# Small experts: gate and up split over TensorE's column quarters by output column, with a buffer and PSUM banks of their own

## The chip, the core and the metric

One core of a Trainium2 chip runs the program. The metric is the device time of one execution in microseconds; the kernel before was timed in three runs. One further execution was profiled, and every row below is from it.

## What is computed

Two decoder layers on 256 tokens of width 1024, all in float32. The part that the change touches is the channel sub-layer of the second layer, a top-2-of-8 mixture of SwiGLU experts with D_FF = 2816:

```
logits = h @ router;  top_val, top_idx = top_k(logits, 2);  gate = softmax(top_val) scattered over 8 experts
out = sum over e of  gate[:, e] * ((silu(h @ w_gate[e]) * (h @ w_up[e])) @ w_down[e])
x   = layer_norm(alpha * x + (1 + g2) * out)
```

## The kernel before

The experts' weights lie in HBM as `moe_units`: 33 units of 1 MB for each expert, that is, for each of the 11 blocks `b` of 256 hidden columns two units of gate and up (one per half of the 1024 rows, laid out as row tile, gate or up, column) and one of down. All 264 units are streamed once, through a ring of 7 buffers of 1 MB that SyncE (SP) fills in order (`moe_raw`, L1404; its DMAs are issued at L1411 and L1416). SP waits at each issue until the buffer's last reader is done.

The router sorts the experts by tokens and picks one of six written-out programs (`PLANS`). The rows below are from the first: three large experts (place 7 with room for 128 tokens, places 0 and 1 with 192) and five small ones (places 6 to 2, 32 tokens each, in the code `WHOLE`). A plan's last tuple says how many slots of small experts are woven into each large expert: 12, 72 and 72 of the 165; what is left runs behind the last large expert. A slot is half a unit of a large expert or a whole unit of a small one.

`experts` (L1776) writes the instructions out in that order under `manual_schedule`. It walks through the slots; ahead of each it calls `tick`, which lets every open generator write one more step. The generators in `procs` (one `glu` per block) all advance; those in `back` only the first (`back_whole`, `scatter_whole`, `scatter` wait in line there), and one `gather` beside them. A generator that finds no scratch bank (`banks`, class Banks) or no room (`t2`, `backs`, `yys`) writes nothing in that tick. Where a slot cannot go on, `until` calls `tick` over and over, and all that the generators then write stands on the engines ahead of the slot.

Large experts: ScalarE copies each half unit to rounded float32 (L1930), VectorE subtracts to get the rest (L1933), and TensorE makes two or three products of 512 columns per token tile (`products`, L1612: L1615, L1616, L1618). Sums lie in banks B and C. `empty` copies a finished expert's four down sums to four buffers `yy` (L1688, then GpSimd at L1690) and `scatter` adds them to the tokens' rows (L1705 to L1722). The next large expert's first product waits until `empty` is written (`full`).

Small experts, in plain float32, which TensorE runs as two passes for each matmul:

- `work_whole` (L1959), gate and up: four matmuls for a unit, one per row tile `a`, each with 32 stationary columns (the tokens) and 512 moving ones, on the four column quarters of the array (L1969). Each quarter so holds a part of the sum over rows for all 512 columns; the four parts must still be added.
- `glu_whole` (L1537): ScalarE copies the 128x512 bank (L1543), four matmuls with `ident4` add the four quarters and turn them (L1549), ScalarE takes silu (L1553), VectorE multiplies by up (L1555).
- down (L1978): four matmuls of 512 columns on the four quarters, into a bank of tag A. The two A banks take turns.
- `empty_whole` (L2038) multiplies the sum by the gain into one of the four `yy` (L2042), `back_whole` (L1566) builds the rows that carry the tokens back (VectorE L1575 and L1579, four transposes L1588, ScalarE L1593) and needs a `yy` too while it does, and `scatter_whole` (L1597) makes four matmuls of 128x512 (L1605), each followed by VectorE's add (L1608).

The four `yy` are thus shared between `empty` (all four at once for 192 tokens), `empty_whole` and `back_whole`. Scratch banks are D and, when no small gate/up sum needs it soon, one B.

`end` (L1725) adds the last small expert (L1736, L1740), normalises and writes out. `rest` (L2226) scales and shifts the residual on GpSimd (L2231, eight instructions of 128x512).

Of the kernel before, what the change touches and what calls it, by code (L numbers as in the profile page):

```python
# [18 lines left out]
D = 1024  # L19
KT = 8  # L20
# [83 lines left out]
class Trunk:  # L104
    def __init__(self, tc, ctx, io):
# [6 lines left out]
        self.aside = 0  # L112

    def bank(self, tag="B"):
        return self.ps.tile([128, 512], F32, tag=tag, name="bank" + tag, bufs={"A": 2, "B": 3, "C": 2, "D": 1}[tag])
# [1133 lines left out]
    def open_moe(self, mo):  # L1249
        self.mx = mo  # L1250
        self.nt2 = 3
# [10 lines left out]
        self.chunks = [c[:, i] for i in range(4)] + [mo.tile([128, KT, 128], F32R, name="xg2")]  # L1262

# [5 lines left out]
    def moe_consts(self):  # L1269
# [12 lines left out]
        nc.vector.tensor_reduce(self.ident4, self.ident.rearrange("p (g n) -> p n g", n=WHOLE), axis=AX.X, op=OP.add)  # L1282
        self.rw = cp.tile([128, KT, 8], F32, name="rw")
# [144 lines left out]
    def gather(self, wanted, xH, xL, out, pos=None, banks=None, t2=None, backs=None):  # L1428
# [58 lines left out]
        for s, w, ch in tiles:  # L1487
# [10 lines left out]
            t = mx.tile([128, SEQ], F32R, tag="selT", name="selT", bufs=8)  # L1498
# [67 lines left out]
    def back_whole(self, place, out, banks, backs, yys):  # L1566
# [5 lines left out]
        while not yys.take():  # L1572
            yield
        sel = self.sums().rearrange("p (t n) -> p t n", t=NT)
        nc.vector.memset(sel, 0.0)  # L1575
        for tt in range(NT):
            for hf in range(2):
                s = sel[:, tt, 128 * hf:128 * hf + 128].rearrange("p (i h n) -> p i h n", h=2, n=WHOLE)[:, :, hf, :]
                nc.vector.tensor_scalar(s, self.iota[:, 0:WHOLE].unsqueeze(1).to_broadcast([128, 2, WHOLE]),  # L1579
# [773 lines left out]
```

## Time and profile before

| | |
|---|---|
| timed runs | 1449.87, 1452.04, 1452.89 us; median 1452.04 |
| profiled execution | 1455.61 us, its span 1453.8 us |
| busy in the span: TensorE, VectorE, ScalarE, GpSimd | 91%, 58%, 43%, 16% |
| granted TensorE clock, mean | 0.956 of full speed |
| moved by DMA | 398.31 MB, 274 GB/s over the span |
| experts, first product to the end | 688.7 to 1453.8 us |

How to read it: the expert part is half the span, and it has stages with different limits, so shares of the whole span say little. The windows below cut it where the large experts begin and end. A row of the view of windows gives, for each stretch, its length, the busy time and instruction count of each engine, the granted clock, the mean busy share of the 16 DMA engines and GB/s. In the timeline, a matmul's time is its latency; how fast matmuls follow each other is read from their starts. A float32 matmul counts as two (a transpose as one).

### The profile page before, as it was taken

The page shows a single profiled execution, that of the slowest core. Times are in us where ns is not written, and L with a number is a line of the kernel's source. Part 1 is how long each engine was busy: PE and PEld are TensorE (multiplying, and loading weights), DVE is VectorE, ACT ScalarE, POOL GpSimd, SP SyncE. Part 2 cuts the span into 40 slices and gives each one's busy share as a digit, 9 for nine tenths or more (in the row PEclk, how much of TensorE's full clock was granted, in tenths as well). Part 3 has the DMA queues.
Part 4 walks back from the last instruction along what each step waited for, and adds up shares of the span by engine and source line. Part 5 has one row for each costly group of instructions (what it writes and reads, how often), then busy time and mean ns, then how long its engine had stood idle before and what let it go on. Part 6 is the DMA issues. An engine that isn't in the chain of part 4 may idle for free.

```text
span 1453.8 us, 21710 instructions
## 1 busy us (share of the span) xinstructions
PE 1329.3 (91%) x8070; PEld 929.4 (64%) x8070; DVE 844.9 (58%) x1691; ACT 621.6 (43%) x1179; POOL 232.5 (16%) x284
## 2 busy tenths in 40 slices
PE   5599998799999789997899999999998999999974
PEld 1457746789998567556677666666655666665622
DVE  7956568987776575656867644444434444444224
ACT  2342544455554314633676534344334344443311
POOL 5562015234000331012300100000002000000012
PEclk9799999899999899998999999999999999999977
DMA  9465743356666648533699999999994999999930
GB/s 328 126 180 161 263 112 119 117 189 219 230 232 203 189 144 277 202 95 138 219 354 375 420 418 417 414 404 410 421 421 174 382 411 412 393 422 398 415 124 31
DMA packets 123969, 398.31 MB, mean 274 GB/s; under 512 B 21256, under 2 KB 74848, under 8 KB 84944
## 3 DMA queue, kind: packets, MB, share of 16 engines
q1 hardware_dynamic: 123248, 396.21, 72.7%
q8 instruction: 65, 1.06, 0.3%
q0 software_dynamic: 608, 0.64, 0.2%
q14 instruction: 48, 0.39, 0.1%
HBM read 395.77 MB, written 1.05 MB: 273 GB/s over the span
## 4 chain that ended last, share of the span: by engine, by line
PE 39%; issue 10%; DVE 2%; POOL 1%; ACT 1%; ACTq 0%; POOLq 0%; DVEq 0%
PE bankB L1615 5%; PE bankB L1616 5%; PE bankC L1615 4%; PE bankC L1969 4%; PE bankC L1616 4%; PE bankB L1618 4%; PE bankA L1978 3%; PE bankB L1969 2%; PE bankC L1618 1%; PE bankD L1549 1%; PE bankB L1549 1%; PE bankB L1526 0%; PE bankD L1716 0%; PE bankD L1643 0%; DVE sel L1513 0%
## 5 line engine op out<-in xcount | busy, mean ns | idle before, releaser
L147 DVE TENSOR_TENSOR L<-raw,H 128x512 fp32r<-128x512 f32 (+1 forms) x241 | 167.3, 706 | 68.2 <-ACT H L143 66.2
L143 ACT ACTIVATE H<-raw 128x512 fp32r<-128x512 f32 (+1 forms) x244 | 144.4, 602 | 134.7 <-PE bankB L153 84.4
L1933 DVE TENSOR_TENSOR early<-raw,early 128x1024 fp32r<-128x1024 f32 x120 | 146.4, 1234 | 89.1 <-ACT early L1930 86.4
L153 PE MATMUL bankB<-hHL,H 128*128 128x256 f32 (+1 forms) x560 | 162.2, 290 | 11.7 <-DVE hHL L395 11.7
L152 PE MATMUL bankB<-hHL,H 128*128 128x256 f32 (+1 forms) x560 | 161.8, 290 | 9.5 <-ACT hHL L394 9.5
L154 PE MATMUL bankB<-hHL,L 128*128 128x256 f32 (+1 forms) x560 | 162.7, 291 | 4.3 <-DVE L L147 4.2
L1930 ACT ACTIVATE early<-raw 128x1024 fp32r<-128x1024 f32 x120 | 123.8, 1050 | 13.1 <-DMA raw<-in_moe_units_dram 9.1
L153 PEld LDWEIGHTS bankB<-hHL,H 128*128 128x128 f32 (+1 forms) x560 | 107.0, 191 | 16.9 <-DVE hHL L395 13.6
L152 PEld LDWEIGHTS bankB<-hHL,H 128*128 128x128 f32 (+1 forms) x560 | 106.6, 191 | 15.2 <-ACT hHL L394 9.8
L1615 PE MATMUL bankB<-early,xg 128*128 128x512 f32 x264 | 113.6, 430 | 1.7 <-ACT xg L1481 1.7
L154 PEld LDWEIGHTS bankB<-hHL,L 128*128 128x128 f32 (+1 forms) x560 | 107.0, 191 | 8.9 <-DVE L L147 5.5
L1616 PE MATMUL bankB<-early,xg 128*128 128x512 f32 x264 | 105.2, 399 | 1.0 <-DVE early L1933 1.0
L1618 PE MATMUL bankB<-early,xg 128*128 128x512 f32 x264 | 105.0, 398 | 0.0
L1615 PEld LDWEIGHTS bankB<-early,xg 128*128 128x128 f32 x264 | 50.1, 190 | 59.1 <-issue 29.5
L1690 POOL TENSOR_TENSOR yy<-yy,grow 128x512 f32<-128x512 f32 x10 | 12.6, 1280 | 388.9 <-ACT yy L1688 388.9
L1615 PE MATMUL bankC<-early,xg 128*128 128x512 f32 x176 | 69.5, 395 | 0.0
L1616 PE MATMUL bankC<-early,xg 128*128 128x512 f32 x176 | 69.5, 395 | 0.0
L1933 DVE TENSOR_TENSOR early<-early,early 128x1024 fp32r<-128x1024 f32 x42 | 52.3, 1262 | 25.3 <-ACT early L1930 23.7
L284 PE MATMUL bankD<-raw,cpad 128*32 128x512 f32 x320 | 54.8, 657 | 6.2 <-DMA raw<-in_ada_w_dram 5.8
L1618 PEld LDWEIGHTS bankB<-early,xg 128*128 128x128 f32 x264 | 50.0, 189 | 11.9
L1933 DVE TENSOR_TENSOR early<-ring,early 128x1024 fp32r<-128x1024 f32 x32 | 40.8, 1285 | 28.2 <-ACT early L1930 27.2
L1615 PE MATMUL bankC<-early,eHL 128*128 128x512 f32 x132 | 56.9, 431 | 0.1
(602 smaller groups left out, 2825.3 us busy)
## 6 DMA issues: line engine op xcount, KB each, us to landing
raw<-in_moe_units_dram SPq DMA_DIRECT2D x151, 1024.0 KB, 8.5
early<-in_moe_units_dram SPq DMA_DIRECT2D x76, 1024.0 KB, 8.6
raw<-in_ada_w_dram SPq DMA_DIRECT2D x48, 1024.0 KB, 5.9
ring<-in_moe_units_dram SPq DMA_DIRECT2D x37, 1024.0 KB, 9.0
raw<-in_ffn_w_gate_dram SPq DMA_DIRECT2D x11, 1024.0 KB, 5.3
raw<-in_ffn_w_up_dram SPq DMA_DIRECT2D x11, 1024.0 KB, 5.1
raw<-in_ffn_w_down_dram SPq DMA_DIRECT2D x11, 1024.0 KB, 6.4
raw<-in_w_in_dram SPq DMA_DIRECT2D x16, 512.0 KB, 5.5
```

The source lines that it names most:

```text
L143: i = nc.scalar.activation(Hv, src, AF.Copy)
L147: self.parts = i, (engine or nc.vector).tensor_sub(Lv, src, Hv.bitcast(F32))
L152: mm(out, lh, rh, start=start, stop=False)
L153: mm(out, lh, rl, start=False, stop=False)
L154: self.last = mm(out, ll, rh, start=False, stop=stop)
L284: nc.tensor.matmul(pt[32 * q:32 * q + 32, :], self.cpad[:, k, :], t[:, 512 * q:512 * q + 512], start=(k == 0), stop=(k == KT - 1))
L1615: mm(o, xs[0], wH, start=first, stop=False)
L1616: mm(o, xs[0], wL, start=False, stop=last and w == 64)
L1618: mm(o, xs[1], wH, start=False, stop=last)
L1930: nc.scalar.activation(zv, src, AF.Copy)
L1933: (nc.gpsimd if not whole and n >= len(slots) - 54 and n % 3 == 2 else v).tensor_sub(zv, src, hl[n][1].bitcast(F32))
L1969: nc.tensor.matmul(o.gu[WHOLE * a:WHOLE * a + WHOLE].rearrange("p (g n) -> p g n", g=2), xs[:, 4 * u + a, c:c + WHOLE], t[:, :, a, :], sta ...
```

## The change

Gate and up of a small expert: each quarter now takes 64 of the 256 output columns of both gate and up, for all eight row tiles, so that a unit is 16 matmuls of 128 columns instead of four of 512, and no sum over quarters is left. Gate and up lie side by side on the same partitions. `glu_whole` takes silu out of the bank, multiplies by up, and only then turns the 128x64 product with two matmuls and one copy. The sums of the small experts' down products get a fixed bank V, the second A bank becomes a scratch bank W, and the scaled sum gets a buffer `yw` of its own. `back_whole` builds its rows without a `yy`, from a diagonal matrix, a matmul with ones and a comparison. The shares are 12, 68 and 68. GpSimd's first instruction of `rest` is a copy of one column of `abuf[4]`, which the first large expert's fifth block writes.

```diff
-    ([(7, 128), (0, 192), (1, 192)], [(6, 32), (5, 32), (4, 32), (3, 32), (2, 32)], (12, 72, 72)),
+    ([(7, 128), (0, 192), (1, 192)], [(6, 32), (5, 32), (4, 32), (3, 32), (2, 32)], (12, 68, 68)),
...
-        self.nt2 = 3
+        self.nt2 = 2
...
+        self.late = mo.tile([128, 1], F32, name="late")
...
+        self.slot = cp.tile([128, 2], F32, name="slot")
...
-            t = mx.tile([128, SEQ], F32R, tag="selT", name="selT", bufs=8)
+            t = mx.tile([128, SEQ], F32R, tag="selT", name="selT", bufs=7)
...
-    def glu_whole(self, g, o, banks, t2):
+    def glu_whole(self, g, o, banks):
...
-        while not t2.take():
-            yield
-        z = self.t2([128, 512])
-        nc.scalar.activation(z, g, AF.Copy)
+        z = self.mx.tile([128, 64], F32, tag="zw", name="zw", bufs=2)
+        nc.scalar.activation(z, g[:, 0:64], AF.Silu)
+        yield
+        nc.vector.tensor_mul(z, z, g[:, 64:128])
         yield "read"
...
-        pt = self.bank(bn)[:, 0:4 * WHOLE]
-        for i in range(4):
-            nc.tensor.matmul(pt[:, WHOLE * i:WHOLE * i + WHOLE], z[:, 128 * i:128 * i + 128], self.ident4,
+        pt = self.bank(bn)[:, 0:2 * WHOLE]
+        id4 = self.ident.rearrange("p (i r n) -> p r i n", i=2, r=2)
+        for r in range(2):
+            nc.tensor.matmul(pt[64 * r:64 * r + 64].rearrange("p (i n) -> p i n", i=2), z, id4[:, r],
                              start=True, stop=True)
-        t2.free()
         yield
-        nc.scalar.activation(o, pt[:, 0:2 * WHOLE], AF.Silu)
-        yield
-        nc.vector.tensor_mul(o, o, pt[:, 2 * WHOLE:4 * WHOLE])
+        nc.scalar.activation(o, pt, AF.Copy)
...
-    def back_whole(self, place, out, banks, backs, yys):
+    def back_whole(self, place, out, banks, backs):
...
-        while not yys.take():
-            yield
-        sel = self.sums().rearrange("p (t n) -> p t n", t=NT)
-        nc.vector.memset(sel, 0.0)
+        dg = [self.act.tile([128, 128], F32, tag="dg", name="dg", bufs=2) for _ in range(NT)]
         for tt in range(NT):
...
+            nc.vector.tensor_scalar(dg[tt], self.ident, self.pos[:, tt, place:place + 1], None, op0=OP.mult)
...
+        for tt in range(NT):
+            nc.tensor.matmul(pt[:, 128 * tt:128 * tt + 128], self.ones, dg[tt], start=True, stop=True)
         yield
         for hf in range(2):
-            t = mx.tile([128, SEQ], F32, tag="selT", name="selW", bufs=8)
-            nc.scalar.activation(t, pt[:, 256 * hf:256 * hf + 256], AF.Copy)
+            t = mx.tile([128, SEQ], F32, tag="selT", name="selW", bufs=7)
+            nc.vector.tensor_scalar(t, pt, self.slot[:, hf:hf + 1], None, op0=OP.is_equal)
...
-        banks = Banks("DB", lambda: state["now"], REST)
+
+        self.fixed = {n: self.bank("A") for n in "VW"} if whole else {}
+        step_banks = "DW" if whole else "D"
+        banks = Banks(step_banks + "B", lambda: state["now"], REST)
...
-                for a in range(4):
-                    nc.tensor.matmul(o.gu[WHOLE * a:WHOLE * a + WHOLE].rearrange("p (g n) -> p g n", g=2),
-                                     xs[:, 4 * u + a, c:c + WHOLE], t[:, :, a, :], start=(u == 0), stop=(u == 1))
+                for k in range(4 * u, 4 * u + 4):
+                    for i in range(4):
+                        nc.tensor.matmul(o.gu[WHOLE * i:WHOLE * i + WHOLE, 0:128].rearrange("p (g n) -> p g n", g=2),
+                                         xs[:, k, c:c + WHOLE], t[:, :, k % 4, 64 * i:64 * i + 64],
+                                         start=(k == 0), stop=(k == KT - 1))
             else:
                 if o.b == 0:
-                    Y[o.q] = self.bank("A")
+                    Y[o.q] = self.bank("V")
...
         def empty_whole(q):
-            while not yys.take(1):
+            while not yw.take():
                 yield
-            y = self.sums()
+            y = self.mx.tile([128, 512], F32, tag="yw", name="yw", bufs=1)
             v.tensor_mul(y, Y[q], gain[0])
...
-            banks.names = "D" if any(o.spare and u == 0 for o, u in soon) else "DB"
+            banks.names = step_banks + ("" if any(o.spare and u == 0 for o, u in soon) else "B")
...
         def rest(banks):
 
+            p.tensor_copy(self.late, self.abuf[4][:, 0:1])
             for tt in range(NT):
```

The change moves instructions. Two places matter.

The first is ScalarE where large expert 0 ends and large expert 1 begins. L1472 and L1481 make the tokens of expert 1 ready (`gather`), L1930 rounds a half unit of weights, L1688 empties expert 0's sums. In the kernel before, from the last silu of the small experts on, no half unit is rounded between these steps:

```order
L1553 ACTIVATE sab<-bankB 128x64
L1472 ACTIVATE t_9847<-bankB,colB,colA 128x192 x2
L1481 ACTIVATE xg<-t_9847 128x256
L1481 ACTIVATE xg<-t_9847 128x2x64
L1472 ACTIVATE t_9866<-bankB,colB,colA 128x192 x2
L1481 ACTIVATE xg<-t_9866 128x256
L1481 ACTIVATE xg<-t_9866 128x2x64
L1593 ACTIVATE selW<-bankD 128x256 x2
```

In the changed kernel the same steps (L1484, L1493) stand well ahead of that place, during expert 0's down products, with the rounding (here L1937) and the small experts' silu (L1554) and copy (L1566) between them:

```order
L1484 ACTIVATE t_9753<-bankA,colB,colA 128x192 x2
L1554 ACTIVATE zw<-bankB 128x64
L1493 ACTIVATE xg<-t_9753 128x256
L1493 ACTIVATE xg<-t_9753 128x2x64
L1937 ACTIVATE early_6727<-ring 128x1024 x2
L1681 ACTIVATE eHL<-ab_6741 128x2x128
L1566 ACTIVATE sab<-bankD 128x64
L1681 ACTIVATE eHL<-ab_6741 128x2x64
L1937 ACTIVATE early_6727<-early_6729 128x1024
L1554 ACTIVATE zw<-bankB 128x64
```

The gather of expert 1 moved from one lump at the handover into the stage of expert 0.

The second is TensorE behind the last product of the last large expert. Before, it carries back two small experts (L1588, L1605) ahead of the next units of weights (L1969 gate and up, L1978 down):

```order
L1978 MATMUL bankA<-raw,sab 32x512 x4
L1549 MATMUL bankD<-ident_2373,t_11796 128x32 x4
L1588 MATMUL bankD<-ident,yy_6727 128x128 x4
L1605 MATMUL bankD<-yy_6726,selW 128x512 x4
L1588 MATMUL bankD<-ident,yy_6725 128x128 x4
L1605 MATMUL bankD<-yy_6724,selW 128x512 x4
L1969 MATMUL bankB<-raw,xg_7065 32x512 x8
L1716 MATMUL bankD<-yHL,selT 128x256 x4
L1978 MATMUL bankA<-ring,sab 32x512 x4
L1716 MATMUL bankD<-yHL,selT 128x256 x4
```

Changed, units of weights (L1977, L1987) come at once, and the large expert's scatter (L1719) stands between them:

```order
L1563 MATMUL bankD<-ident,zw 64x64 x2
L1977 MATMUL bankB<-early_6729,xg_7075 32x128 x16
L1977 MATMUL bankB<-raw,xg_7075 32x128 x16
L1719 MATMUL bankD<-yHL,selT 128x256 x4
L1987 MATMUL bankA<-raw,sab 32x512 x4
L1563 MATMUL bankA<-ident,zw 64x64 x2
L1719 MATMUL bankD<-yHL,selT 128x256 x4
L1977 MATMUL bankB<-raw,xg_7075 32x128 x16
L1977 MATMUL bankB<-ring,xg_7075 32x128 x16
L1719 MATMUL bankD<-yHL,selT 128x256 x4
```

The carrying back of the small experts (L1608 in the changed kernel) moved forward, four instructions for each expert spread between products of the large ones, and 17 units instead of 9 are left for this last stretch.

## Rows read from the trace of the kernel before

**Rows 1.** The page: the span, busy time of the engines, and GB/s in 40 equal slices of the span.

```profile
span 1453.8 us, 21710 instructions
...
PE 1329.3 (91%) x8070; PEld 929.4 (64%) x8070; DVE 844.9 (58%) x1691; ACT 621.6 (43%) x1179; POOL 232.5 (16%) x284
...
GB/s 328 126 180 161 263 112 119 117 189 219 230 232 203 189 144 277 202 95 138 219 354 375 420 418 417 414 404 410 421 421 174 382 411 412 393 422 398 415 124 31
```

**Rows 2.** The view of windows: the expert part cut into expert 7 (two rows), expert 0, the handover, expert 1, the stop behind it, the last units, and `end`.

```profile
688.70:704.00 15.30, 9.37 (x37) 6.72 (x38) 11.10 (x13) 8.61 (x9) 13.20 (x8) 0.92 0.23 72
704.00:823.40 119.40, 119.40 (x626) 87.36 (x625) 86.61 (x118) 82.33 (x131) 5.13 (x6) 0.98 0.94 363
823.40:1086.60 263.20, 261.86 (x1504) 167.06 (x1500) 114.35 (x175) 106.43 (x184) 4.86 (x5) 1.00 1.01 415
1086.60:1113.20 26.60, 19.91 (x106) 12.95 (x102) 13.32 (x38) 12.59 (x33) 3.53 (x3) 0.94 0.36 151
1113.20:1382.00 268.80, 266.19 (x1525) 170.66 (x1521) 108.47 (x167) 105.47 (x186) 8.85 (x10) 0.99 0.98 399
1382.00:1411.30 29.30, 19.45 (x56) 6.14 (x55) 7.46 (x14) 4.51 (x11) 5.67 (x5) 0.71 0.23 86
1411.30:1434.90 23.60, 17.13 (x98) 8.94 (x97) 5.77 (x16) 4.42 (x12) 5.08 (x7) 0.80 0.17 71
1434.90:1453.80 18.90, 5.70 (x8) 2.19 (x8) 11.00 (x18) 1.01 (x2) 5.71 (x6) 0.68 0.16 59
```

**Rows 3.** The timeline of TensorE in the stage of expert 0, where a product, a down unit, a `glu_whole`, a gate/up unit and the next product follow each other (start, length, line, shapes, count).

```profile
967.26 1.06 PE L1978 MATMUL bankA<-raw,sab 128*32 128x512 f32 x8
...
968.26 1.08 PE L1549 MATMUL bankD<-ident,t 128*128 128x32 f32 x8
...
969.27 1.06 PE L1969 MATMUL bankC<-ring,xg 128*32 128x512 f32 x8
...
970.26 0.50 PE L1615 MATMUL bankB<-early,xg 128*128 128x512 f32 x1
```

**Rows 4.** The view of windows, stage of expert 0, for the matmuls of line 1549 alone and then of line 1978 alone (eight records per block, and per unit).

```profile
823.40:1086.60 263.20, 22.96 (x184) 23.08 (x184) 1.00 1.01 415
...
823.40:1086.60 263.20, 25.39 (x192) 4.19 (x192) 1.00 1.01 415
```

**Rows 5.** The timeline of ScalarE and VectorE around the same place: silu, multiplication and the copy of a bank in `glu_whole`.

```profile
961.52 0.22 ACT L1553 ACTIVATE sab<-bankB 128x64 f32<-128x64 f32 x1 [0.43 <-PE bankB L1549]
961.77 0.22 DVE L1555 TENSOR_TENSOR sab<-sab,bankB 128x64 f32<-128x64 f32 x1 [1.45 <-ACT sab L1553]
...
962.62 0.60 ACT L1543 ACTIVATE t<-bankC 128x512 f32<-128x512 f32 x1 [0.88 <-PE bankC L1969]
```

**Rows 6.** The timeline of TensorE, three runs of short float32 passes elsewhere in the program: 128 columns in one quarter, 64 columns in two halves, 128 columns in two halves.

```profile
73.34 1.72 PE L684 MATMUL bankC<-early,X 128*32 128x128 f32 x14
...
244.79 1.15 PE L617 MATMUL bankD<-ident,sl 128*64 128x64 f32 x32
...
1102.80 0.66 PE L1495 MATMUL bankB<-ident,sel 128*64 128x128 f32 x8
```

**Rows 7.** The view of windows, the handover from expert 0 to 1, for lines 1458 (`gather`), 1526 (`gather_whole`) and 1605 (`scatter_whole`, two records each) alone.

```profile
1086.60:1113.20 26.60, 4.83 (x32) 3.96 (x32) 0.94 0.36 151
...
1086.60:1113.20 26.60, 4.59 (x24) 4.42 (x24) 0.94 0.36 151
...
1086.60:1113.20 26.60, 7.86 (x14) 2.09 (x14) 0.94 0.36 151
```

**Rows 8.** The timeline at the start of expert 7: GpSimd's `rest`, one of TensorE's waits, and VectorE's subtraction (L1933) and comparison (L1513, four at a time) first beside `rest` and then without it.

```profile
688.74 13.20 POOL L2231 TENSOR_TENSOR x<-x,yy 128x512 f32<-128x512 f32 x8 [15.88 <-ACT xg L1481]
...
695.20 0.50 PE L1616 MATMUL bankB<-early,xg 128*128 128x512 f32 x1 [0.42 <-DVE early L1933]
...
697.30 2.31 DVE L1933 TENSOR_TENSOR early<-raw,early 128x1024 fp32r<-128x1024 f32 x1
699.53 2.75 DVE L1513 TENSOR_SCALAR sel<-iota,posS 128x32 fp32r<-128x32 f32 x4
702.19 1.22 DVE L1933 TENSOR_TENSOR early<-raw,early 128x1024 fp32r<-128x1024 f32 x1
...
703.66 0.67 DVE L1513 TENSOR_SCALAR sel<-iota,posS 128x32 fp32r<-128x32 f32 x4
```

**Rows 9.** The view of waits of SP's DMA queue over the expert part: who was waited for, microseconds in total, times, longest; and the timeline of SP at the handover.

```profile
SPq L1411 <- PE bankC L1969: 49.8, 10, 26.0
...
SPq L1416 <- PE bankB L1969: 44.9, 10, 26.2
...
1086.13 27.63 SPq L1411 DMA_DIRECT2D raw<-in_moe_units_dram  x3
```

**Rows 10.** The timeline behind the last product of the last large expert, and from the view of DMA issues the median from issue to landing of a unit.

```profile
1381.88 27.12 SPq L1416 DMA_DIRECT2D raw<-in_moe_units_dram  x2
...
1384.78 1.12 PE L1605 MATMUL bankD<-yy,selW 128*128 128x512 f32 x2 [0.75 <-ACT selW L1593]
...
1406.71 2.67 PE L1969 MATMUL bankB<-raw,xg 128*32 128x512 f32 x16
...
1427.18 0.58 PE L1716 MATMUL bankD<-yHL,selT 128*128 128x256 f32 x1 [0.57 <-ACT yHL L1705]
...
1429.57 0.58 PE L1716 MATMUL bankD<-yHL,selT 128*128 128x256 f32 x1 [0.57 <-ACT yHL L1705]
...
1434.88 3.78 PE L1740 MATMUL bankB<-yy,selW 128*128 128x512 f32 x4 [0.47 <-ACT selW L1593]
...
raw<-in_moe_units_dram SPq DMA_DIRECT2D x130, 1024.0 KB, 8.8
```

More of the change, by code (lines that the diff above doesn't have):

```diff
@@ L112, in __init__ @@
         self.aside = 0
+        self.fixed = {}
     def bank(self, tag="B"):
+        if tag in self.fixed:
+            return self.fixed[tag]
         return self.ps.tile([128, 512], F32, tag=tag, name="bank" + tag, bufs={"A": 2, "B": 3, "C": 2, "D": 1}[tag])
@@ L1282, in moe_consts @@
         nc.vector.tensor_reduce(self.ident4, self.ident.rearrange("p (g n) -> p n g", n=WHOLE), axis=AX.X, op=OP.add)
+        self.slot = cp.tile([128, 2], F32, name="slot")
+        t = self.mx.tile([128, 512], F32, tag="asb", name="asb", bufs=1)[:, 0:WHOLE]
+        nc.vector.tensor_mul(t, self.ident4, self.iota[:, 0:WHOLE])
+        for hf in range(2):
+            nc.vector.tensor_reduce(self.slot[:, hf:hf + 1], t, axis=AX.X, op=OP.add)
+        for i in range(128 // WHOLE):
+            nc.vector.memset(self.slot[WHOLE * i:WHOLE * i + WHOLE, 1 - i % 2:2 - i % 2], -2.0)
         self.rw = cp.tile([128, KT, 8], F32, name="rw")
@@ L1571, in back_whole @@
             yield
-        while not yys.take():
-            yield
-        sel = self.sums().rearrange("p (t n) -> p t n", t=NT)
-        nc.vector.memset(sel, 0.0)
+        dg = [self.act.tile([128, 128], F32, tag="dg", name="dg", bufs=2) for _ in range(NT)]
         for tt in range(NT):
-            for hf in range(2):
-                s = sel[:, tt, 128 * hf:128 * hf + 128].rearrange("p (i h n) -> p i h n", h=2, n=WHOLE)[:, :, hf, :]
-                nc.vector.tensor_scalar(s, self.iota[:, 0:WHOLE].unsqueeze(1).to_broadcast([128, 2, WHOLE]),
-                                        self.pos[:, tt, place:place + 1], None, op0=OP.is_equal)
+            nc.vector.tensor_scalar(dg[tt], self.ident, self.pos[:, tt, place:place + 1], None, op0=OP.mult)
         yield
@@ L1583, in back_whole @@
             yield
-        pt = self.bank(bn)
-        for hf in range(2):
-            for tt in range(NT):
-                c = 256 * hf + 128 * tt
-                nc.tensor.transpose(pt[:, c:c + 128], sel[:, tt, 128 * hf:128 * hf + 128], self.ident)
-        yys.free()
+        pt = self.bank(bn)[:, 0:SEQ]
+        for tt in range(NT):
+            nc.tensor.matmul(pt[:, 128 * tt:128 * tt + 128], self.ones, dg[tt], start=True, stop=True)
         yield
         for hf in range(2):
-            t = mx.tile([128, SEQ], F32, tag="selT", name="selW", bufs=8)
-            nc.scalar.activation(t, pt[:, 256 * hf:256 * hf + 256], AF.Copy)
+            t = mx.tile([128, SEQ], F32, tag="selT", name="selW", bufs=7)
+            nc.vector.tensor_scalar(t, pt, self.slot[:, hf:hf + 1], None, op0=OP.is_equal)
             out.append(t)
@@ L1853, in experts @@
                 continue
-            kinds = {z.kind for z, _ in slots[max(o.first - NEAR, 0):o.last + NEAR] if z.q in large}
+            kinds = {z.kind for z, _ in slots[max(o.first - NEAR - (AHEAD if whole else 0), 0):o.last + NEAR]
+                     if z.q in large}
             o.spare = kinds != {"u"}
@@ L1895, in experts @@
         place = {n: i for i, n in enumerate([n for n, (o, _) in enumerate(slots) if o.q not in whole])}
-        selW, gain = {}, []
+        selW, gain, yw = {}, [], Room(1)
         procs = []
@@ L1994, in glu @@
             if o.q in whole:
-                work = self.glu_whole(o.gu, parts(o.q, o.b), banks, t2)
+                work = self.glu_whole(o.gu, parts(o.q, o.b), banks)
             else:
@@ L2048, in scatter_whole @@
             yield from self.scatter_whole(q, selW[q], ys[q], acc, banks)
-            yys.free(1)
+            yw.free()
             backs.free(2)
@@ L2115, in after @@
                     if o.b == NB - LATE:
-                        back.append(self.back_whole(o.q, selW.setdefault(o.q, []), banks, backs, yys))
+                        back.append(self.back_whole(o.q, selW.setdefault(o.q, []), banks, backs))
                 elif o.b == NB - 1:
```

2 lines of the change are left out of this document (1 added, 1 removed).

## Prediction

> **What bounds the kernel now.** I read the page first and then the expert part in windows. TensorE is busy for 91% of the span, but the GB/s line says more: from the 23rd slice on it stands near 415, with one hole in the 31st and an end that moves little [rows 1]. So two engines are near full at once. The windows show it stage by stage [rows 2]. In the stage of expert 0 (263.2 us) TensorE is busy for 261.9 us and the DMA engines for the whole of it at 415 GB/s; in that of expert 1 (268.8 us) it is 266.2 us and 399 GB/s. Between and behind them lie two holes: 26.6 us at 151 GB/s at the handover, 29.3 us at 86 GB/s behind the last large product. There the stream of weights stands: SP's two longest waits, 26.0 and 26.2 us, are for gate/up matmuls of small experts [rows 9], which hold the ring's oldest buffers and stand on TensorE behind work that has nothing to do with weights [rows 10]. Then 23.6 us of last units and 18.9 us of `end`.
>
> What sets the pace inside a stage? The reader should compare starts: down unit 967.26, `glu_whole` 968.26, gate/up unit 969.27, product 970.26 [rows 3]. They follow each other without a gap, 1.0 us each. TensorE is thus the one that others wait for, with the DMA right behind: a stage of 72 slots and 33 large units takes in 105 units of 1.049 MB, which at 415 GB/s need 265 us.
>
> All sums below are against the profiled execution; its 1455.61 us are 3.6 us above the median of the timed runs, 1452.04, to which I apply the difference.
>
> **The change part by part.**
>
> *Gate and up, 110 units.* One unit was 4 matmuls of 512 columns on four quarters: 8 passes, 0.99 us from start to next start [rows 3]. Now it is 16 matmuls of 128 columns, 32 passes; each quarter streams 4 x 128 columns as it streamed 512. If the quarters still run at once, the streaming is the same, and only more weight loads and issues could show. No row has 128 columns on four quarters. Near it: 32 passes with their 32 loads took 1.15 us where each was 64 columns on halves [rows 6], so the engine can issue that many in about a microsecond; that is the upper near bound, +0.16 us. The lower bound is a few hundredths below nothing, since the drain at either end is shared. Far bounds: one at a time, 1.72 us for 14 passes, 0.12 a pass and 3.9 us a unit; two at a time half of that, 2.0 us (8 passes on halves took 0.66 us with their latency, 0.08 a pass) [rows 6]. I take +0.05 us, nearest to the four-quarter row, whose geometry it keeps.
>
> *`glu_whole`, 55 blocks.* Eight passes with loads of 128 columns took 1.0 us [rows 3], 22.96 us of busy time for 23 blocks in one stage [rows 4]; where a product follows, about 0.9. Now 4 passes of 64 columns on halves: at the 0.036 us a pass of line 617 [rows 6] 0.14 us, and a change of array shape on both sides for which I add 0.2. I take 0.35, bounds 0.15 and 0.9. ScalarE gives up a 0.60 us copy and gains a 0.22 us one [rows 5]; VectorE's product stays. Both are busy for about 40% of these stages [rows 2], so neither costs anything; if they were full, it would be the 0.2 us of the added copy a block.
>
> *Start of expert 7, 15.3 us.* GpSimd's eight instructions run at 688.74 for 13.2 us, and beside them VectorE's subtraction takes 2.31 instead of 1.22 us and four comparisons 2.75 instead of 0.67; TensorE waits for the subtraction [rows 8] and is busy for 9.4 of 15.3 us [rows 2]. The copy of one column holds GpSimd back until the fifth block is through, some 30 us later, when VectorE has run ahead. I take -5 us here. The rest of expert 7's stage: 5 `glu_whole` save 2.8, ten gate/up units cost 0.5, the moved GpSimd work 1: **-1.3** (bounds -3 and +4, if all of the slowness moves along).
>
> *Stage of expert 0, 263.2 us.* Less: four slots of about 0.95 us, 3.8; 23 `glu_whole` of 0.91 become 22.7 of 0.35, 13.0. More: 45 gate/up units, 2.3. And the work of the handover now lies in here: the gather of expert 1, 4.8 us, that of the last small expert, 4.6, seven products of `scatter_whole` in 14 records, 7.9 [rows 7], less some 0.6 since the clock was 0.94 there and will be 1.00; the selection matrices 1.3 and `back_whole` 0.5. Sum **+3.2**. Its DMA floor is 101 units, 255 us; TensorE still sets the pace with 266.
>
> *Handover.* 26.6 us become the wait for expert 0's sums to leave their banks, two copies, 1.5 us: **-25.1**. The order of the changed kernel shows why nothing else is left: two scratch banks instead of one, and `empty` no longer queues for four buffers behind the small experts' sums.
>
> *Stage of expert 1, 268.8 us.* The same -3.8, -13.0 and +2.3; one gather bank falls out, -1.1; two small experts' `scatter_whole` move in, eight products of 1.06, +8.5, and two `back_whole`, +1. Sum **-6.1**; floor again 255.
>
> *Behind the last large product.* 29.3 + 23.6 = 52.9 us become a stretch of 17 units with the large expert's eight scatter steps between them. By landing: 8.8 us from issue to landing [rows 10] is 3.5 units of 2.53 us, so of the ring's seven some 3.5 have landed and 13.5 are to come, 34 us, and 1.7 for the last down and the gain. By TensorE: ten gate/up units 10.5, seven down 7, six `glu_whole` 2, eight scatter steps of 2.4 us, the distance of two of them [rows 10], 19: 38.6. I take 38: **-15** (bounds -19 and -5). `end` stays 18.9.
>
> Sum: -5 - 1.3 + 3.2 - 25.1 - 6.1 - 15 = **-49.3 us**, and 1452.04 - 49.3 = 1402.7; I say **1402**. The seven small VectorE instructions that build `slot` lie in the first layer's stage and change the order there a little; at the 0.2 us of such instructions this is 1.4 us if bare, and I count it as nothing with 3 us to either side.
>
> **Rivals.**
>
> *A. The DMA becomes the bound.* If `glu_whole` takes 0.15 and gate/up nothing more, TensorE falls to 255 us a stage and below, and the stages cannot be shorter than their bytes: -11, -8 and in the last stretch -3 from my forecast, **1380**. For it: 415 GB/s at full share [rows 2]. Against: TensorE still has 250 us of work a stage by my sum. No cheaper TensorE brings more than this.
>
> *B. A queue comes back.* V is one bank and `yw` one buffer: the next small expert's first down unit waits for VectorE to empty V, and that for the last carrying back. A wait of 2 us at four handovers of small experts, plus half of the old stop at expert 1 because its first product still needs a bank: +8 and +12, **1422**.
>
> *C. Slower: the short passes do not share the array.* Place: every gate/up unit. If passes of 128 columns run only two at a time, as the rows on halves show, a unit takes 2.0 us, 0.9 more than I take, 110 units, nearly all in stages that TensorE paces: +99, **1501**. It decides from the point where a unit costs 0.45 us more than forecast, that is 1.5 us, 47 ns a pass. For it: no row shows four at once at this length. Against: the 512-column rows show four at once, 8 passes in a microsecond [rows 3]; and line 617 makes 32 passes with their loads at 36 ns [rows 6].
> The Trainium skill, page "TensorE: Matmul & The Clock Gate", section "Back-to-back issue gap", speaks for C: in a stream of load and matmul pairs it gives about 81 ns a matmul of 128 columns. By that estimate 32 passes take 2.6 us, and the kernel would stand near 1570 us. The trace disagrees for passes that share the array (36 ns a pass for line 617 [rows 6]), which is why C keeps a small chance.
>
> **How the numbers follow.** Forecast 0.60, A 0.16, B 0.14, C 0.10. About 0.2% (3 us) is what a measurement of this kernel can tell from no change. Forecast, A and nearly all of B are faster: 0.89; 0.02 for a C or B that just eats the gain; slower 0.09. The range runs from A's 1380 to 1430, which takes in B, gate/up at the 1.15 us bound (100 units x 0.11 = +11) and the last stretch at its bound (+10) together; C stays outside.
>
> **What would show it.** Right: TensorE's gate/up units start 1.0 to 1.1 us apart, `glu_whole` takes under 0.5; GB/s has no hole between the stages and stays above 390 until some 40 us before the end; TensorE's first 36 products take about 10 us; SP has no wait over 15 us in the expert part. Wrong: gate/up units above 1.2 us (C), a stretch below 300 GB/s at the handover (B), or TensorE waiting for landings through the stages (A).

## The result, and the profile after

The changed kernel takes 1398.91 us (median of four runs, 1394.03 to 1399.67) against 1452.47 us for the kernel before: 0.962 of it, 95% interval 0.9585 to 0.9655, 53.6 us less, where 50 were forecast. The profiled execution took 1399.39 us, its span 1397.7 us.

The page of the changed kernel, to be read against [rows 1]: TensorE is still busy for 91% of a shorter span. The hole in the line of GB/s is gone, and the stream runs, with dips, the lowest to 351, up to the last of the 40 slices.

```profile
span 1397.7 us, 26504 instructions
...
PE 1278.2 (91%) x10490; PEld 951.2 (68%) x10490; DVE 846.5 (61%) x1693; ACT 595.6 (43%) x1169; POOL 237.3 (17%) x285
...
GB/s 322 139 151 174 252 122 150 120 183 211 194 246 223 181 164 217 265 127 163 120 315 359 405 419 419 419 384 407 419 383 351 392 379 397 383 417 420 410 420 186
```

The windows of the changed kernel (columns as in [rows 2]), cut at products: the first 36 of expert 7, the rest of it, expert 0, the handover, expert 1, the stretch behind the last large product, and `end`.

```profile
685.60:695.20 9.60, 8.63 (x36) 6.68 (x36) 6.13 (x12) 7.87 (x10) 0.00 (x0) 1.00 0.23 76
695.20:813.00 117.80, 115.70 (x871) 88.86 (x871) 94.04 (x119) 81.50 (x133) 21.54 (x15) 1.00 0.93 365
813.00:1080.00 267.00, 259.80 (x2522) 188.13 (x2522) 124.17 (x207) 104.59 (x207) 5.37 (x6) 1.00 0.99 401
1080.00:1081.80 1.80, 1.80 (x41) 0.98 (x40) 1.69 (x2) 1.80 (x5) 1.66 (x2) 1.00 0.89 350
1081.80:1342.50 260.70, 252.95 (x2460) 182.00 (x2458) 116.40 (x178) 96.20 (x184) 12.25 (x12) 1.00 0.99 399
1342.50:1378.70 36.20, 27.32 (x437) 16.48 (x437) 6.56 (x18) 6.83 (x22) 9.86 (x12) 0.91 0.93 383
1378.70:1397.70 19.00, 5.45 (x8) 2.07 (x8) 10.99 (x18) 0.81 (x1) 5.72 (x6) 0.68 0.16 58
```

The 27 us of the handover are 1.8. Read the third and fifth rows again, though: TensorE is idle for 7.2 and 7.8 us in these stages, where it was idle for 1.3 and 2.6 in [rows 2], the DMA share is 0.99, and yet the rate is 401 and not 415 GB/s. Which of the two sets the pace is not plain from here; an experiment settles it.

The timeline of TensorE in the stage of expert 0, at the place that answers to [rows 3]: `glu_whole`, a down unit, a gate/up unit, the next product, and the transposes of the large expert's 64-token tile.

```profile
962.98 0.34 PE L1563 MATMUL bankA<-ident,zw 128*64 128x64 f32 x4
963.24 1.07 PE L1987 MATMUL bankA<-ring,sab 128*32 128x512 f32 x8
964.12 1.06 PE L1977 MATMUL bankC<-early,xg 128*32 128x128 f32 x32
965.11 0.50 PE L1618 MATMUL bankB<-early,xg 128*128 128x512 f32 x1
...
970.71 0.66 PE L1646 MATMUL bankD<-ident,t 128*128 128x128 f32 x4 [0.69 <-ACT t L1635]
```

By starts, the gate/up unit takes 965.11 - 964.12 = 0.99 us, to the hundredth what it took in [rows 3], with four times as many matmuls. `glu_whole` takes 0.26 us instead of 1.0. The last row shows a wait that has grown: TensorE waits for ScalarE's copy of the 64-token tile (`t`) before it can turn it. The view of TensorE's waits over the expert part (total, times, longest):

```profile
PE bankD L1646 <- ACT t L1635: 6.9, 12, 0.7
PE bankA L1646 <- ACT t L1635: 3.4, 8, 0.4
PE bankA L1987 <- DMA raw<-in_moe_units_dram: 2.7, 2, 1.5
...
PE bankB L1646 <- ACT t L1635: 0.4, 1, 0.4
```

The wait for the copy is 10.7 us in all. In the kernel before the same wait (there L1643 on L1632) came to 2.1 us:

```profile
PE bankD L1643 <- ACT t L1632: 1.4, 2, 0.7
...
PE bankB L1643 <- ACT t L1632: 0.7, 2, 0.5
```

SP's longest wait in the expert part is now 5.8 us, not 26 [rows 9]:

```profile
SPq L1423 <- DVE early L1940: 119.0, 42, 5.8
SPq L1423 <- PE bankC L1977: 87.4, 28, 5.5
```

The timeline behind the last large product, answering to [rows 10]: gate/up (L1977), the large expert's scatter (L1719), down (L1987).

```profile
1355.80 1.08 PE L1977 MATMUL bankB<-raw,xg 128*32 128x128 f32 x32
1356.70 1.06 PE L1977 MATMUL bankB<-early,xg 128*32 128x128 f32 x32
1357.68 0.73 PE L1719 MATMUL bankD<-yHL,selT 128*128 128x256 f32 x4
1358.35 1.06 PE L1987 MATMUL bankA<-raw,sab 128*32 128x512 f32 x8
...
1368.21 1.08 PE L1977 MATMUL bankB<-raw,xg 128*32 128x128 f32 x32 [1.30 <-DMA raw<-in_moe_units_dram]
...
1373.28 1.07 PE L1987 MATMUL bankA<-raw,sab 128*32 128x512 f32 x8 [1.51 <-DMA raw<-in_moe_units_dram]
```

A scatter step takes 0.67 us by starts here, not the 2.4 us of [rows 10], since units of weights stand between the steps and cover what each waits for; one of the eight still waits, 2.3 us for GpSimd. At the end TensorE waits for landings.

### The profile page after: what moved, and what is told of

Read it like the earlier page. It is cut to its first block, busy times and chain, and to the rows that moved or that the text cites. A ratio compares the mean times of both kernels' runs of the same rounds, so it can differ in the third digit from the quotient of the medians.

```text
span 1397.7 us, 26504 instructions
## 1 busy us (share of the span) xinstructions
PE 1278.2 (91%) x10490; PEld 951.2 (68%) x10490; DVE 846.5 (61%) x1693; ACT 595.6 (43%) x1169; POOL 237.3 (17%) x285
## 4 chain that ended last, share of the span: by engine, by line
PE 46%; DVE 2%; POOL 1%; issue 1%; ACT 1%; DMA 1%; DVEq 0%; POOLq 0%; ACTq 0%
PE bankB L1618 6%; PE bankB L1619 6%; PE bankC L1618 5%; PE bankC L1619 5%; PE bankB L1621 4%; PE bankC L1977 4%; PE bankA L1987 4%; PE bankB L1977 3%; PE bankC L1621 2%; DMA raw<-in_moe_units_dram 1%; ACT t L1635 1%; POOL yy L1693 1%; PE bankA L1608 1%; PE bankD L1646 1%; PE bankD L1666 1%
## 5 line engine op out<-in xcount | busy, mean ns | idle before, releaser
L1940 DVE TENSOR_TENSOR early<-raw,early 128x1024 fp32r<-128x1024 f32 x106 | 131.2, 1254 | 53.2 <-ACT early L1937 40.4
L1937 ACT ACTIVATE early<-raw 128x1024 fp32r<-128x1024 f32 x106 | 109.1, 1051 | 1.1 <-PE bankB L1621 1.0
L1693 POOL TENSOR_TENSOR yy<-yy,grow 128x512 f32<-128x512 f32 x10 | 15.4, 1564 | 498.3 <-ACT yy L1691 498.2
L1940 DVE TENSOR_TENSOR early<-early,early 128x1024 fp32r<-128x1024 f32 x58 | 73.6, 1282 | 33.6 <-ACT early L1937 27.5
L1618 PEld LDWEIGHTS bankB<-early,xg 128*128 128x128 f32 x264 | 49.6, 188 | 32.7 <-issue 17.1
L1937 ACT ACTIVATE early<-early 128x1024 fp32r<-128x1024 f32 x58 | 60.1, 1052 | 3.4 <-PE bankB L1621 3.4
L1621 PEld LDWEIGHTS bankB<-early,xg 128*128 128x128 f32 x264 | 49.6, 188 | 11.8
L1619 PEld LDWEIGHTS bankB<-early,xg 128*128 128x128 f32 x264 | 49.7, 188 | 9.3 <-issue 1.0
```

What stands on the lines that cost most here:

```text
L1618: mm(o, xs[0], wH, start=first, stop=False)
L1619: mm(o, xs[0], wL, start=False, stop=last and w == 64)
L1621: mm(o, xs[1], wH, start=False, stop=last)
L1937: nc.scalar.activation(zv, src, AF.Copy)
L1940: (nc.gpsimd if not whole and n >= len(slots) - 54 and n % 3 == 2 else v).tensor_sub(zv, src, hl[n][1].bitcast(F32))
```

## The experiments

The table has every kernel that was run. The lengths are us between products in each profiled execution: expert 7, expert 0, the handover, expert 1, and from the last large product to the matmuls of `end`. The time is the median of the runs, with its ratio to the kernel before and the 95% interval.

| kernel | exp. 7 | exp. 0 | handover | exp. 1 | behind | time, us | ratio |
|---|---|---|---|---|---|---|---|
| before | 134.7 | 262.2 | 27.6 | 267.5 | 54.1 | 1452.47 | 1 |
| changed | 127.4 | 267.0 | 1.8 | 260.7 | 36.2 | 1398.91 | 0.962 (0.9585 to 0.9655) |
| split_alone | 132.8 | 256.6 | 29.0 | 269.7 | 29.5 | 1424.18 | 0.980 (0.977 to 0.983) |
| scratch_alone | 135.4 | 274.8 | 8.7 | 276.2 | 27.4 | 1429.61 | 0.984 (0.980 to 0.987) |
| split_and_banks | 132.9 | 269.8 | 3.0 | 262.5 | 27.8 | 1404.15 | 0.967 (0.966 to 0.969) |
| queues_alone | 129.1 | 273.3 | 8.4 | 271.6 | 36.7 | 1424.59 | 0.982 (0.978 to 0.985) |
| shared_yy | 127.4 | 267.0 | 1.8 | 260.8 | 35.0 | 1397.77 | 0.961 (0.958 to 0.965) |
| one_scratch_bank | 127.0 | 248.1 | 23.2 | 253.8 | 45.6 | 1406.23 | 0.968 (0.966 to 0.971) |
| no_late | 132.6 | 267.0 | 1.8 | 260.7 | 35.5 | 1401.43 | 0.963 (0.960 to 0.966) |
| fewer_products | 118.0 | 252.9 | 1.8 | 250.0 | 42.0 | 1371.05 | 0.942 (0.939 to 0.946) |
| same_quarter | 140.9 | 324.2 | 3.2 | 316.5 | 37.5 | 1527.01 | one execution |
| shares72 | 127.5 | 269.5 | 3.0 | 262.2 | 28.6 | 1395.07 | 0.959 (0.956 to 0.963) |
| late_turn | 127.3 | 263.4 | 1.8 | 257.9 | 34.9 | 1389.17 | 0.956 (0.953 to 0.959) |
| late_turn_72 | 127.3 | 266.4 | 3.0 | 260.3 | 29.7 | 1391.56 | 0.957 (0.954 to 0.960) |

**Which part of the change gives what.** First the split without the rest, and the rest without the split.

split_alone is the kernel before with the new `glu_whole` and the new loops, both whole as in the change:

```diff
-    def glu_whole(self, g, o, banks, t2):
+    def glu_whole(self, g, o, banks):
...
-                for a in range(4):
...
+                for k in range(4 * u, 4 * u + 4):
+                    for i in range(4):
...
```

> The kernel before with the new gate/up split and the new glu_whole only (and two rooms for t2 instead of three); one scratch bank, shared yy, shares 12, 72, 72 and GpSimd's early start stay. Theory 1, TensorE paces the stages and every shorter glu_whole is time: 55 blocks x 0.65 us (0.91 before, 0.26 now) = 36 us, 1452 - 36 = 1416, with the two holes of 26 and 29 us still there. Theory 2, the stream of weights is the second wall right behind: a stage of 105 units of 1.049 MB needs 265 us at 415 GB/s and took 263.2 and 268.8, so only expert 7 (-3), the stage of expert 1 (-3) and the last units (-3) gain, 1443.

queues_alone is the changed kernel with the same lines turned back.

> The changed kernel with the old split of gate and up by row tile and the old glu_whole; its own buffer and banks, the shares 12, 68, 68 and GpSimd's late start stay. Theory 1, TensorE paces the stages: the 36 us of the split come back whole, 1399 + 36 = 1435, stages near 285 and 272 us, no hole between them. Theory 2, the stream paces the stages: little comes back, 5 us in expert 7 and 5 in the last stretch, 1409.

Measured: 1424.18 and 1424.59 (the profiled execution of queues_alone was 6.6 us below its median, but its expert part began at 680.1 us, 5.5 us sooner than in the changed kernel, so that most of this lies ahead of the lengths in the table), both between the two theories. The rows of split_alone say why (windows: expert 0, handover, expert 1, behind):

```profile
820.20:1076.80 256.60, 253.34 (x2545) 180.32 (x2548) 116.76 (x185) 98.01 (x186) 4.43 (x5) 1.00 1.01 420
1076.80:1105.80 29.00, 18.92 (x111) 13.09 (x108) 11.30 (x16) 11.04 (x28) 8.75 (x9) 0.74 0.59 238
1105.80:1375.50 269.70, 264.11 (x2584) 189.56 (x2586) 116.50 (x194) 99.03 (x194) 3.41 (x5) 0.98 0.94 385
1375.50:1405.00 29.50, 19.19 (x216) 10.80 (x216) 5.77 (x16) 5.89 (x18) 9.87 (x12) 0.88 0.55 227
```

In the stage of expert 0, TensorE lost some 15 us of `glu_whole` (22.96 us [rows 4] became 7.71) and the stage only 5.6. Part of the saving was filled at once: carrying back moved into the stages from the holes behind them. The matmuls of `scatter_whole` alone, stage of expert 0 and the stretch behind the last large product, in the kernel before (L1605) and then in split_alone (L1604):

```profile
823.50:1085.70 262.20, 1.12 (x2) 0.30 (x2) 1.00 1.01 415
...
1380.80:1434.90 54.10, 13.28 (x16) 3.19 (x16) 0.75 0.22 87
```

```profile
820.20:1076.80 256.60, 5.21 (x10) 1.73 (x10) 1.00 1.01 420
...
1375.50:1405.00 29.50, 0.00 (x0) 0.00 (x0) 0.88 0.55 227
```

So TensorE's busy time in the stage of expert 0 fell by 7.5 us, and it idles for 3.3 us instead of 1.3, 2.1 of it for landings, with the stream at 420 GB/s. Both engines are near full there; how much of the lost saving is the stream's is not told apart. The handover, with less in it, is no shorter: it still holds 19 us of TensorE's work, at a clock of 0.74, and 10 us of idling instead of 6.7. Of the 28.5 us that the lengths of split_alone sum to less, 24.6 lie behind the last large product. Theory 1 is wrong for this kernel, theory 2 nearly right for its stages; both had missed that the hole at the end goes.

**Buffer or bank.** shared_yy takes the own buffer back, one_scratch_bank the second scratch bank:

```diff
-            while not yw.take():
+            while not yys.take(1):
...
-            y = self.mx.tile([128, 512], F32, tag="yw", name="yw", bufs=1)
+            y = self.sums()
...
-            yw.free()
+            yys.free(1)
```

> The changed kernel with the small experts' scaled sum in one of the four yy again instead of its own yw; banks V and W stay. Theory 1, the queue for the four yy made the holes: the one at the handover comes back with some 25 us and the last stretch grows by some 12, 1436, SP's longest wait above 15 us. Theory 3, the single scratch bank made them: 1402, no hole.

```diff
-        self.fixed = {n: self.bank("A") for n in "VW"} if whole else {}
-        step_banks = "DW" if whole else "D"
+        self.fixed = {}
+        step_banks = "D"
...
-                    Y[o.q] = self.bank("V")
+                    Y[o.q] = self.bank("A")
```

> The changed kernel with one scratch bank: the small experts' down sums take turns in the two A banks as before, and W is gone; the own buffer yw stays. Theory 1, the queue for the four yy made the holes: near 1402, no hole. Theory 3, the single scratch bank made them, since generators that find no bank write nothing and are written in one lump where the next expert stops: a hole of 15 to 25 us comes back, 1420 or more.

Measured: without `yw` nothing changes (1397.77). Without W the hole is back, 23.2 us, as theory 3 said, but the time grows by 7.3 us and not by 20:

```profile
813.10:1061.20 248.10, 248.10 (x2432) 178.07 (x2432) 116.11 (x181) 95.12 (x179) 5.43 (x6) 1.00 1.01 419
1061.20:1084.40 23.20, 19.14 (x123) 13.79 (x120) 9.58 (x19) 11.80 (x32) 8.57 (x11) 0.78 0.68 283
```

The hole is full of work, 19.1 us of TensorE's 23.2, and what lies in it has left the stage ahead, which is 18.9 us shorter than in the changed kernel. A hole costs what TensorE idles in it and what the lower clock adds, not its length. The 7.3 us are a net figure, though. Expert 0 and the hole together are 2.5 us longer than in the changed kernel, expert 1 is 6.9 shorter, and the stretch behind is 9.4 longer; and the wait for ScalarE's copy, 10.7 us in the changed kernel, is 1.4 here. Against late_turn (below), which has neither the hole nor that wait, expert 0 with the hole is 6.1 us longer. An estimate from the row gives 4.1 us of idling and 4.2 for a clock of 0.78 over 19.1 us. V and W come and go together in these runs, so a fixed bank and a second scratch bank are not told apart.

scratch_alone puts V and W into the kernel before, and nothing else:

```diff
...
-        banks = Banks("DB", lambda: state["now"], REST)
+        self.fixed = {n: self.bank("A") for n in "VW"} if whole else {}
+        step_banks = "DW" if whole else "D"
+        banks = Banks(step_banks + "B", lambda: state["now"], REST)
...
-                    Y[o.q] = self.bank("A")
+                    Y[o.q] = self.bank("V")
...
```

> The kernel before with the banks alone: V for the small experts' down sums, W as a second scratch bank; the split by row tile, glu_whole, the shared yy and the shares 12, 72, 72 stay. If the single scratch bank made the hole at the handover, it goes (27.6 us from the last product of expert 0 to the first of expert 1), and of its 19.9 us of TensorE's work some 18.5 lie in the stage before: net 6 to 8 us, 1445. If the queue for the four yy made it, the hole stays and so does the time, 1452.

Measured: 1429.61, a gain of 23 us and not 7. The handover did as expected (262.2 + 27.6 = 289.8 became 274.8 + 8.7 = 283.5). The rest came from the end: expert 1 grew by 8.7 us, the stretch behind it fell from 54.1 to 27.4:

```profile
1381.60:1409.00 27.40, 20.34 (x133) 10.22 (x133) 5.99 (x17) 6.58 (x18) 9.88 (x12) 0.90 0.47 192
```

In the kernel before, TensorE idled for 10 of that hole's 29.3 us, and its clock was 0.71 [rows 2]; the steps of a carrying back stood there one behind the other, with no unit of weights between them. With the split or with the banks the carrying back of the small experts is written earlier, and either alone is enough at this place: neither kernel has a matmul of `scatter_whole` behind the last large product, where the kernel before has 16 records. So their gains there cannot add up, and yet 28 and 23 make up nearly the whole 53.6. split_and_banks, both in the kernel before, was to tell why:

> The kernel before with two parts of the change: the split with its glu_whole (two rooms for t2), and the banks V and W. Shared yy, back_whole with transposes, shares 12, 72, 72 and GpSimd's early start stay. Alone the split gave 28 us and the banks 23, both of it mostly behind the last large expert (54 us to 29.5 and 27.4), which cannot be won twice. If the split's saving inside the stages is won only once the lump at the handover lies in the stage (alone, the stage of expert 0 went from 262.2 to 256.6 us at 420 GB/s), both together give expert 7 133, expert 0 with its handover 272, expert 1 262, the rest 29: 696 instead of 746 and 1403. If the parts are mere substitutes, 1422. If the yy or the new back_whole are needed, a hole of over 8 us stays at the handover and the time lies near 1412.

Measured: 1404.15, and 132.9, 269.8 + 3.0, 262.5, 27.8 in the table, each within 1.2 us of the expectation:

```profile
821.20:1091.00 269.80, 263.82 (x2618) 189.98 (x2619) 124.13 (x212) 107.53 (x213) 5.29 (x6) 1.00 1.01 414
1091.00:1094.00 3.00, 3.00 (x52) 2.00 (x51) 1.24 (x1) 2.46 (x7) 2.86 (x3) 1.00 0.81 295
```

Over expert 0 with its handover, split and banks alone win 4.2 and 6.3 us and together 17.0, 6.5 more than the sum; over expert 1 with the stretch behind it, 22.4 and 18.0 and together 31.3, 9.1 less. The two interactions nearly cancel. Once the lump of the handover lies in the stage as TensorE's work, the split's saving there is won; that the stream was the wall without it is argued from the 420 GB/s of split_alone and not shown by a run of its own. These two parts are 48 of the 53.6 us. The own `yw`, the new `back_whole`, the shares and GpSimd's late start are the other 5 together.

**What paces the stages now.** fewer_products leaves out, for the tiles of 128 tokens, the third product, that is, the rest of the tokens times the rounded weights:

```diff
-        mm(o, xs[0], wL, start=False, stop=last and w == 64)
-        if w == 128:
-            mm(o, xs[1], wH, start=False, stop=last)
+        mm(o, xs[0], wL, start=False, stop=last)
```

> The changed kernel without the third product of each 128-token tile (the rest of the tokens times the rounded weights is left out): 220 products of 0.22 us fewer in each stage of a 192-token expert, 132 of them... counted from the trace of the changed kernel, 134 records of L1621 a stage, 29 us of TensorE. If TensorE paces the stages, they shrink until the stream stops them, 101 units x 2.5 us (1.049 MB at 419 GB/s) = 252 us, from 267 and 261: 1375, and the stream's rate goes from 400 to 415 GB/s or more. If the stream is held at 400 GB/s by something of its own, the stages stay within 3 us, 1395.

```profile
807.80:1060.70 252.90, 234.30 (x2386) 163.03 (x2382) 120.85 (x207) 106.07 (x207) 4.42 (x6) 0.99 1.01 419
...
1062.50:1312.50 250.00, 226.12 (x2326) 155.96 (x2323) 115.67 (x179) 98.01 (x185) 11.67 (x12) 1.00 1.01 419
```

Measured: 1371.05. The stages shrink to 252.9 and 250.0 us and stop there, with TensorE idle for 19 and 24 us and the stream at 419 GB/s. TensorE, with its waits, paces the changed kernel's stages; the stream is 11 to 14 us behind it. The DMA share does not tell the two apart: it was 0.99 at 401 GB/s and 1.01 at 419.

**What rival C would have been.** same_quarter exchanges the two loops of gate and up:

```diff
-                for k in range(4 * u, 4 * u + 4):
-                    for i in range(4):
+                for i in range(4):
+                    for k in range(4 * u, 4 * u + 4):
```

> The changed kernel with the two loops of gate and up exchanged: four row tiles into one column quarter, then the next quarter, so that matmuls that follow each other stand on the same quarter. If quarters run side by side only where neighbours in the order are on different ones, a unit of 32 passes goes from 0.9 us to 2 us at the least and up to 3.9 us (0.12 us a pass): 1399 + 110 = 1510 or more. If the order does not matter, 1399.

```profile
970.72 2.44 PE L1977 MATMUL bankC<-raw,xg 128*32 128x128 f32 x32
973.09 0.50 PE L1618 MATMUL bankB<-early,xg 128*128 128x512 f32 x1
```

Measured: 1527 us, and a unit of 2.37 us by starts, 74 ns a pass against 31 in the order of the change. The very same 32 passes differ only in whether neighbours stand on the same quarter. The Trainium skill's 81 ns for a load and matmul of 128 columns (page "TensorE: Matmul & The Clock Gate", section "Back-to-back issue gap") fits this kernel within a tenth, and not the changed one.

**The new wait.** late_turn writes the transposes of the 64-token tile one step of its generator later:

```diff
         for n, z in gs.items():
             w, o = tiles[n][0], ab[n]
+            yield
             while not (bn := banks.take()):
```

> The changed kernel, where the four transposes of a large expert's 64-token tile (L1646) are written one slot later. In the changed kernel TensorE waits for ScalarE's copy ahead of them, 6.9 + 3.4 us in all, where it waited 2.1 us before. If the shorter glu_whole uncovered this wait, it goes: TensorE's stages shrink by 8 us in all, 1391. If TensorE does not pace the stages, or the wait only moves, 1399.

```profile
811.50:1074.90 263.40, 262.07 (x2521) 186.55 (x2517) 123.87 (x207) 104.39 (x207) 5.40 (x6) 1.00 1.00 407
...
1076.70:1334.60 257.90, 255.98 (x2460) 180.23 (x2456) 116.50 (x179) 96.10 (x184) 12.26 (x12) 1.00 0.99 403
```

Measured: 1389.17, 9.7 us less than the changed kernel, 8 of it in the table (the two intervals just touch, so the reading rests on the rows too); the wait has no row any more, and TensorE is idle for 1.3 and 1.9 us in these stages instead of 7.2 and 7.8. The reason in the expectation was wrong, though. The wait is 2.1 us in split_alone, which has the short `glu_whole`, and 7.1 in scratch_alone, which does not; with one_scratch_bank it is 1.4 (the rows of the wait, one block for each kernel in this order):

```profile
PE bankD L1642 <- ACT t L1631: 1.4, 2, 0.7
...
PE bankB L1642 <- ACT t L1631: 0.7, 1, 0.7
```

```profile
PE bankD L1646 <- ACT t L1635: 6.4, 10, 0.7
...
PE bankA L1646 <- ACT t L1635: 0.7, 1, 0.7
```

```profile
PE bankD L1646 <- ACT t L1635: 1.4, 2, 0.7
```

It is the second scratch bank that brings it: a generator that always finds a bank writes the transposes one slot sooner, before ScalarE's copy is through.

**Shares and GpSimd.** shares72 turns the shares back to 12, 72, 72:

> The changed kernel with the old shares 12, 72, 72: nine units behind the last large expert instead of 17, four more in each stage. If TensorE paces the stages, four units add some 4 us to each and the last stretch (36 us from the last product to the final matmuls) gives back more than 8: 1390. If the stream paces everything, each unit costs the same 2.5 us wherever it stands: 1399. If the eight scatter steps then lie bare at the end: slower, 1405.

Measured: 1395.07, whose interval overlaps that of the changed kernel. Eight units less behind the last expert save 7.6 us there and cost 5.2 in the stages and the handover. Together with the later transposes:

> The changed kernel with both: transposes one slot later, and the shares 12, 72, 72. If the two gains are independent (10 us and 4 us, the second within its interval), 1385. If the second was only scatter, 1389.

Measured: 1391.56, not below late_turn alone. The shares are thus worth nothing that these runs can tell. no_late drops GpSimd's copy:

```diff
-            p.tensor_copy(self.late, self.abuf[4][:, 0:1])
```

> The changed kernel without GpSimd's copy of one column ahead of rest. If the two engines' overlap is what slows the start of expert 7, the subtractions of some 1.2 us there take above 2 us again and the first 36 products 15 us instead of 10: 1404. If other parts of the change had made the start shorter, 1399.

VectorE's timeline at the start of expert 7, without the copy:

```profile
694.03 2.31 DVE L1940 TENSOR_TENSOR early<-raw,early 128x1024 fp32r<-128x1024 f32 x1
696.26 2.75 DVE L1525 TENSOR_SCALAR sel<-iota,posS 128x32 fp32r<-128x32 f32 x4
```

and in the changed kernel:

```profile
691.89 1.22 DVE L1940 TENSOR_TENSOR early<-raw,early 128x1024 fp32r<-128x1024 f32 x1
693.03 0.67 DVE L1525 TENSOR_SCALAR sel<-iota,posS 128x32 fp32r<-128x32 f32 x4
```

The durations beside `rest` are those of [rows 8], and expert 7 takes 132.6 instead of 127.4 us. The medians differ by 2.5 us, within the intervals, so 5 us rests on the two profiles. The overlap is not gone in the changed kernel but moved to 728 us, where a subtraction takes 2.32 us again and TensorE is busy all the same (VectorE's timeline, and the window of all engines):

```profile
729.64 2.32 DVE L1940 TENSOR_TENSOR early<-raw,early 128x1024 fp32r<-128x1024 f32 x1
```

```profile
726.00:743.00 17.00, 16.58 (x140) 12.80 (x138) 17.00 (x13) 13.39 (x27) 15.71 (x9) 1.00 0.85 318
```

## Why the prediction was right

- **What bounds the kernel.** Right: TensorE paces the stages with the stream close behind. Rival A's wall was put at 255 us a stage; fewer_products met it at 250 to 253.
- **Gate and up, +0.05 us a unit.** Nothing was lost (0.99 and 0.99). The quarters do run at once with 128 columns, as the four-quarter row of [rows 3] said; rival C is false in the order that the change has. Its far bound, 0.12 us a pass one at a time, was put too high: same_quarter shows 74 ns.
- **`glu_whole`, 0.35 us.** It is 0.26, so 55 blocks save some 5 us more than said. The waits for the 64-token tile's copy, which the prediction did not have, took 8.6 back (10.7 us against 2.1). The sum was right partly by luck, since these two errors cancel.
- **Start and rest of expert 7, -5 and -1.3.** 134.7 to 127.4, -7.3; no_late shows 5.2 of it.
- **Expert 0 with the handover, -21.9.** 289.8 to 268.8, -21.0. The terms written out for the stage add up to +4.0 and not to +3.2, which would have made it -21.1. The size held because the work that left the hole was charged to the stage. Of the two reasons given, the second scratch bank (with V) is right, and the queue for the four `yy` is not: shared_yy has no hole.
- **Expert 1, -6.1.** 267.5 to 260.7, -6.8.
- **Behind the last product, -15.** 54.1 to 36.2, -17.9. The sum by landings (35.7) was right and that by TensorE (38.6) mis-sized: a scatter step costs 0.67 us between units, not 2.4.
- **The rest.** `end` is 19.0 for 18.9. The expert part begins 3 us sooner (685.6 for 688.7), within the 3 us left open; in the profiles of the variants it begins anywhere from 680.1 to 689.8 us, so no gain is shown there. From the first product to `end` the terms sum to -53.0 against -49.3.
- **Signs.** The 36 products took 9.6 us, SP's longest wait was 5.8 us (so no queue of rival B), and the handover moved 350 GB/s. One sign failed: the rate was to stay above 390 and sagged to 351 in the stages, where SP waits above all for TensorE's gate/up matmuls to give the ring's buffers back; in fewer_products it stays at 417 to 420.
- **What the prediction did not see** is that the terms depend on each other. The split's saving at expert 0 and its handover is won in full only beside the banks (17.0 us against 4.2 and 6.3 alone), and the hole at the end goes with either. The forecast came out all the same, since it priced each stage with all parts of the change in it.

Among the kernels that leave out no product, late_turn has the lowest median, 1389.17 us: 0.956 of the kernel before, against 0.962 for the change.

## What to carry to other kernels

When a queue of postponed work is dissolved, price the work in its new place: a hole is worth its idle time and its low clock, not its length. Two engines near full at once make the gains of separate edits depend on each other, so each edit is priced with the other's wall in the sum. A resource that is suddenly always free moves instructions earlier, and may put them in front of what they wait for; read the list of waits again after it.

## What the runs showed of the hardware

- Matmuls of 128 columns on four column quarters share the array only if neighbours in the order stand on different quarters: 0.99 us a unit of 32 passes against 2.37 us in the other order.
- The mean busy share of the DMA engines was 0.99 at 399 to 401 GB/s and 1.01 at 419: near 1, it does not say that the stream is the limit.
- In a hole, where TensorE stops again and again, the granted clock is on the mean between its levels of 1.2 and 2.4 GHz (0.74 of full in split_alone's handover, 0.78 in one_scratch_bank's, 0.71 in [rows 2]), and the same work takes longer: the kernel with V and W alone has 698.0 us of TensorE busy from the first product to `end`, the kernel before 713.2, with the same matmuls. An estimate from the clock and busy time of each window puts some 10 of these 15 us down to the clock.
